# Rounding and spreading V on GpSimd, straight from fp32, in a softmax-times-V kernel

## Chip, cores, metric

One core of a Trainium2 chip. The metric is the device time of one execution in microseconds (us), lower is better. "Same" means less than 2% of difference.

## The reference

```python
batch, n_heads, seq, head_dim = 8, 12, 1024, 64      # scores 8x12x1024x1024 fp32, v 8x12x1024x64 fp32
attn = np.exp(scores - np.max(scores, axis=-1, keepdims=True))
attn = attn / (np.sum(attn, axis=-1, keepdims=True) + 1e-8)
return np.matmul(attn, v)
```

403 MB of scores, 25 MB of V and 25 MB of output have to cross between device memory and the core.

## The kernel before

The 96 heads run in 24 rounds of four. For each head, ScalarE takes the exponential of the scores (fp16 out; the maximum is not subtracted), TensorE transposes it into PSUM (the memory that its results go to), VectorE copies it back to SBUF (the main on-chip memory; `pt`), and TensorE multiplies with V. V carries a column of ones, so that the same product gives the row sums; VectorE divides by them. All transfers are issued by SyncE (SP in the profile), in program order, on one queue.

V is loaded for four heads at once, as fp32, each head on 32 partitions. GpSimd (POOL) rounds the whole tile to fp16, and VectorE (DVE) spreads each head with four copies onto all 128 partitions of that head's operand `vones`:

```python
v_sb = sb_pool.tile([P, C // L, S, L, D], FP32, name="v_sb")     # 128 x 2048
v_half = sb_pool.tile([P, C // L, S, L, D], FP16, name="v_half")
# vones_bufs: four tiles [P, C, D + 2] fp16, ones in the last columns

def cast_v():
    nc.gpsimd.tensor_copy(out=v_half[:], in_=v_sb[:])

def spread_v(k, s, behind=None):
    copy = nc.vector.tensor_copy(
        out=vones_bufs[k][s * Q : (s + 1) * Q, :, 0:D].rearrange("i (h l) d -> i h l d", l=L),
        in_=v_half[k * Q : (k + 1) * Q, :, s],
    )
    ...

def last(n0):                      # after the round's four heads
    with tc.If(n0 < BH - 2 * AHEAD) as cmp:
        load(AHEAD - 2, ...)       # third head of the next round; the first two were issued earlier
        load_v((n0 + 2 * AHEAD) % BH)
        load(AHEAD - 1, ...)       # fourth head
        store(n0, AHEAD - T)
    ...                            # the last two rounds load no V

def heads(n0):
    for k in range(AHEAD):
        if k == 0:
            for s in range(S):
                spread_v(k, s)
        for r in range(R):
            ...                    # exp, transposes, copy to pt
            if k < AHEAD - 1 and r % (R // S) == 0:
                spread_v(k + 1, r // (R // S), copy)
            ...                    # product of an earlier row group
    ...
    cast_v()
    last(n0)
```

## Time and profile before

| | before |
|---|---|
| time | 1065.75 us (1065.68 to 1065.76, three runs) |
| busy: TensorE, VectorE, ScalarE, GpSimd | 731, 787, 736, 48 us |
| DMA queue | 453 MB, 99.2% of the 16 engines' span |
| a steady round of four heads | 43.7 us, 18.87 MB, 432 GB/s |

In the page, a group's line gives line number, engine, operation, output and input, count, then busy time and mean ns of one, then the engine's idle time before it and what ended it. In a timeline, the first two numbers are start and length in us, and the bracket is the idle time before with what ended it. The lines themselves are in the prediction.

### The profile page before, as it was taken

What the parts mean: (1) busy time and instruction counts of PE and PEld (TensorE: products, weight loads), DVE (VectorE), ACT (ScalarE), POOL (GpSimd) and SP (SyncE); (2) the same over time, 40 slices, a digit from 0 to 9 for tenths busy, and PEclk for the clock granted to TensorE, in tenths of its full rate; (3) what the DMA queues carried; (4) which work ended last, traced back from release to release, by engine and by line L of the source; (5) the groups of instructions that cost most, each with busy time, mean ns of one, the idle gap of its engine ahead of it and who ended that gap; (6) DMA issues with size and microseconds to landing.
All of it is one profiled execution on the core that took longest, in us unless ns stands there. A gap on an engine that the chain in (4) does not pass through costs nothing.

```text
span 1064.0 us, 32161 instructions
## 1 busy us (share of the span) xinstructions
PE 731.4 (69%) x12288; PEld 678.4 (64%) x12288; DVE 786.6 (74%) x1589; ACT 735.6 (69%) x432; POOL 48.1 (5%) x31
## 2 busy tenths in 40 slices
PE   2766766767766677677686776867666777666676
PEld 2665756667666667666575665767565666666675
DVE  3776876868768777677786776868768687687777
ACT  3766776666767668586676866667766668676685
POOL 0000000000000000000000000000000000000000
PEclk9888888878889888888988888888889788898989
DMA  9999999999999999999999999999999999999995
GB/s 397 431 418 434 426 433 434 433 434 432 432 434 432 425 443 430 429 431 428 433 431 436 432 434 434 431 434 424 441 427 434 432 426 435 432 432 428 440 425 236
DMA packets 24772, 453.06 MB, mean 426 GB/s; under 512 B 2752, under 2 KB 2752, under 8 KB 9152
## 3 DMA queue, kind: packets, MB, share of 16 engines
q1 hardware_dynamic: 24768, 453.00, 99.2%
q8 instruction: 4, 0.07, 0.0%
HBM read 436.21 MB, written 25.17 MB: 434 GB/s over the span
## 4 chain that ended last, share of the span: by engine, by line
DMA 81%; ACT 12%; issue 3%; ACTq 1%; PE 1%; DVE 0%; SPq 0%; PEld 0%; DVEq 0%
DMA s_nat<-in_scores_dram 81%; ACT p_nat L255 12%; PE psT L267 1%; ACTq L255 1%; ACTq L226 0%; ACTq L292 0%; PE psO L145 0%; DVE pt L273 0%; PE psO_whole L145 0%; SPq L184 0%; PEld L267 0%; ACTq L320 0%; DVE out_sb L129 0%; SPq L196 0%; PEld L145 0%
## 5 line engine op out<-in xcount | busy, mean ns | idle before, releaser
L255 ACT ACTIVATE p_nat<-s_nat 128x2048 f16<-128x2048 f32 (+1 forms) x408 | 704.8, 1799 | 228.1 <-DMA s_nat<-in_scores_dram 202.2
L267 PE MATMUL psT<-order,p_nat 128*128 128x128 f16 x6144 | 574.9, 246 | 269.9 <-ACT p_nat L255 263.9
L273 DVE COPY pt<-psT 128x1024 f16<-128x1024 f16 x768 | 515.8, 687 | 200.6 <-PE L267 109.4
L267 PEld LDWEIGHTS <-p_nat 128*128 128x128 f16 x6144 | 446.5, 123 | 298.3 <-ACT p_nat L255 295.7
L145 PEld LDWEIGHTS <-pt 128*128 128x128 f16 x6144 | 302.9, 107 | 81.0 <-DVE pt L273 77.7
L145 PE MATMUL psO<-vones,pt 128*128 128x65 f16 x3072 | 177.4, 201 | 53.9 <-DVE pt L273 50.2
L145 PE MATMUL psO_whole<-vones,pt 128*128 128x65 f16 x3072 | 189.9, 211 | 2.7 <-DVE pt L273 2.4
L207 DVE COPY vones<-v_half 32x512 f16<-32x512 f16 x384 | 109.4, 285 | 22.8 <-POOL v_half L203 6.0
L255 ACT ACT_TABLE_LOAD x24 | 30.8, 1283 | 89.8 <-DMA s_nat<-in_scores_dram 81.7
L203 POOL CAST v_half<-v_sb 128x2048 f16<-128x2048 f32 x25 | 47.4, 1896 | 1002.3 <-DVE vones L207 957.1
L129 DVE TENSOR_TENSOR out_sb<-psO,recip 64x256 f32<-64x256 f32 x192 | 81.1, 423 | 6.1
L129 DVE TENSOR_TENSOR out_sb<-psO_whole,recip 64x512 f32<-64x512 f32 x96 | 66.1, 688 | 3.0
L124 DVE RECIPROCAL recip<-psO 128x4 f32<-128x4 f32 x96 | 17.1, 178 | 34.4 <-PE psO L145 17.6
L124 DVE RECIPROCAL recip<-psO_whole 128x8 f32<-128x8 f32 x48 | 9.7, 203 | 4.5 <-PE psT L267 3.9
L71 DVE MEMSET vones<- 128x16 f16 x4 | 0.2, 72 | 0.8 <-PEq L309 0.8
L62 DVE CAST order<-ident 128x128 f16<-128x128 f32 x1 | 0.2, 227 | 0.4 <-POOL ident masks.py:199 0.4
masks.py:199 POOL TENSOR_SCALAR_AFFINE_SELECT ident<-ident 128x128 f32<-128x128 f32 x1 | 0.3, 295 | 0.1
masks.py:197 POOL MEMSET ident<- 128x128 f32 x1 | 0.2, 205 | 0.3 <-POOLq L309 0.3
L309 POOL MEMSET const-float32-0.0<- 128x1 f32 x1 | 0.1, 100 | 0.2 <-issue 0.2
L309 POOL MEMSET const-bfloat16-1.0<- 128x1 bf16 x1 | 0.1, 103 | 0.0
L309 POOL MEMSET const-uint8-127<- 128x1 uint8 x1 | 0.1, 103 | 0.0
L309 POOL MEMSET const-float32-1.0<- 128x1 f32 x1 | 0.1, 100 | 0.0
## 6 DMA issues: line engine op xcount, KB each, us to landing
s_nat<-in_scores_dram SPq DMA_DIRECT2D x96, 4096.0 KB, 35.8
v_sb<-in_v_dram SPq DMA_DIRECT2D x24, 1024.0 KB, 33.1
out_dram<-out_sb SPq DMA_DIRECT2D x48, 512.0 KB, 26.9
s_nat<-in_scores_dram SPq DMA_DIRECT2D x3, 2048.0 KB, 32.4
s_nat<-in_scores_dram SPq DMA_DIRECT2D x1, 1024.0 KB, 25.4
s_nat<-in_scores_dram SPq DMA_DIRECT2D x2, 512.0 KB
```

The costliest lines, as they stand in the source:

```text
L62: nc.vector.tensor_copy(out=order16[:].rearrange("p (t j) -> p t j", t=T), in_=ident32[:].rearrange("p (j t) -> p t j", t=T),)
L71: nc.vector.memset(vo[:, :, D : D + 2], 1.0)
L124: nc.vector.reciprocal(out=recip, in_=psO[:, :, :, D : D + 1])
L129: nc.vector.tensor_tensor(out=rows.rearrange("j (b g) d -> j b g d", g=G), in0=psO[part, :, :, 0:D], in1=recip[part].to_broadcast([W, last ...
L145: nc.tensor.matmul(out=bank[:, g * M : (g + 1) * M], lhsT=pt[:, c * P : (c + 1) * P], rhs=st["vones"][:, c, 0:M], start=(c == 0), stop=(c ...
L203: nc.gpsimd.tensor_copy(out=v_half[:], in_=v_sb[:])
L207: copy = nc.vector.tensor_copy(out=vones_bufs[k][s * Q : (s + 1) * Q, :, 0:D].rearrange("i (h l) d -> i h l d", l=L), in_=v_half[k * Q : ( ...
L255: nc.scalar.activation(out=p_nat[:, g : g + rows, :].rearrange("p r (x v) -> p x r v", v=Q * L), in_=s_bufs[k][:, r + g : r + g + rows, :] ...
L267: nc.tensor.transpose(out=psT[:, c * P : (c + 1) * P], in_=p_row[:, c // L, c % L, :], identity=order16[:],)
L273: copy = nc.vector.tensor_copy(out=pt[:], in_=psT[:])
L309: nc = _bacc.Bacc("TRN2", target_bir_lowering=False, num_devices=1)
```

## The change

Its intent is to take V's handling off VectorE, the busiest engine, and to save the fp16 copy of the tile. GpSimd reads fp32 and writes fp16 into `vones`, four copies a head, after the head's last product.

```diff
-    v_half = sb_pool.tile([P, C // L, S, L, D], FP16, name="v_half")
...
-        if r == R - 1 and k == T - 1:
-            store(n0, 0)
+        if r == R - 1:
+            spread_v(k)
+            if k == T - 1:
+                store(n0, 0)
...
-    def cast_v():
-        nc.gpsimd.tensor_copy(out=v_half[:], in_=v_sb[:])
-    def spread_v(k, s, behind=None):
-        copy = nc.vector.tensor_copy(... in_=v_half[k * Q : (k + 1) * Q, :, s])
+    def spread_v(k):
+        for s in range(S):
+            nc.gpsimd.tensor_copy(... in_=v_sb[k * Q : (k + 1) * Q, :, s])
...
-            if k == 0:
-                for s in range(S):
-                    spread_v(k, s)
...
-                if k < AHEAD - 1 and r % (R // S) == 0:
-                    spread_v(k + 1, r // (R // S), copy)
...
-        cast_v()
         last(n0)
...
-    cast_v()
+    for k in range(AHEAD):
+        spread_v(k)
     load_v(AHEAD)
```

More of the change, by code (lines that the diff above doesn't have):

```diff
@@ L200, in load_v @@
         )
-    def cast_v():
-        nc.gpsimd.tensor_copy(out=v_half[:], in_=v_sb[:])
-    def spread_v(k, s, behind=None):
-        copy = nc.vector.tensor_copy(
-            out=vones_bufs[k][s * Q : (s + 1) * Q, :, 0:D].rearrange(
-                "i (h l) d -> i h l d", l=L
-            ),
-            in_=v_half[k * Q : (k + 1) * Q, :, s],
-        )
-        if behind is not None:
-            after(copy, behind)
+    def spread_v(k):
+        for s in range(S):
+            nc.gpsimd.tensor_copy(
+                out=vones_bufs[k][s * Q : (s + 1) * Q, :, 0:D].rearrange(
+                    "i (h l) d -> i h l d", l=L
+                ),
+                in_=v_sb[k * Q : (k + 1) * Q, :, s],
+            )
     def load_next(k, n0):
@@ L272, in heads @@
                 pt = take(pt_bufs)
-                copy = nc.vector.tensor_copy(out=pt[:], in_=psT[:])
-                if k < AHEAD - 1 and r % (R // S) == 0:
-                    spread_v(k + 1, r // (R // S), copy)
+                nc.vector.tensor_copy(out=pt[:], in_=psT[:])
                 if r == R - 1:
```

## The prediction

> **What bounds the kernel now.** I read the page from the top: busy times, slices, queues, the chain that ended last; then the traffic of one steady round of four heads; then the moments at which SyncE issues its transfers in that round.
>
> The page of the kernel before: busy times, the DMA row of the slices, the queue, the chain by engine, and the two groups that the change removes.
> ```profile
> PE 731.4 (69%) x12288; PEld 678.4 (64%) x12288; DVE 786.6 (74%) x1589; ACT 735.6 (69%) x432; POOL 48.1 (5%) x31
> ...
> DMA  9999999999999999999999999999999999999995
> ...
> q1 hardware_dynamic: 24768, 453.00, 99.2%
> ...
> DMA 81%; ACT 12%; issue 3%; ACTq 1%; PE 1%; DVE 0%; SPq 0%; PEld 0%; DVEq 0%
> ...
> L207 DVE COPY vones<-v_half 32x512 f16<-32x512 f16 x384 | 109.4, 285 | 22.8 <-POOL v_half L203 6.0 <-PE L267 3.2 <-DVE out_sb L129 2.1
> L203 POOL CAST v_half<-v_sb 128x2048 f16<-128x2048 f32 x25 | 47.4, 1896 | 1002.3 <-DVE vones L207 957.1 <-DMA v_sb<-in_v_dram 40.8 <-POOLq L292 4.3
> ```
> No compute engine is over 74% busy; the one queue is at 99.2% and full in every slice but the last. The chain gives DMA 81% and VectorE 0%.
>
> One round (two scores loads, a store, then a third scores load, V, the fourth scores load, a store), busy time by stretch; after the five engines come granted clock, DMA share and GB/s:
> ```profile
> 405.63:449.34 43.71, 30.59 (x504) 28.46 (x501) 32.48 (x67) 30.65 (x18) 1.90 (x1) 0.80 1.00 432
> 449.34:493.02 43.68, 31.55 (x510) 29.44 (x508) 32.73 (x67) 30.64 (x18) 1.90 (x1) 0.80 1.01 432
> ```
> A round moves 4 x 4.194 + 1.049 + 2 x 0.524 = 18.87 MB; over 43.68 us that is 432 GB/s. 24 rounds are 453 MB, 1048.6 us at that rate; the other 15 us or so are first transfer and tail.
>
> SyncE's timeline for the same round, then its longest waits (total, times, longest us):
> ```profile
> 437.92 0.34 SPq L184 DMA_DIRECT2D s_nat<-in_scores_dram  x1
> 442.85 0.33 SPq L196 DMA_DIRECT2D v_sb<-in_v_dram  x1
> 449.34 0.33 SPq L184 DMA_DIRECT2D s_nat<-in_scores_dram  x1
> 456.05 0.36 SPq L163 DMA_DIRECT2D out_dram<-out_sb  x1
> ```
> ```profile
> SPq L184 <- ACT p_nat L255: 273.4, 47, 13.1
> ...
> SPq L226 <- SPq L226: 129.6, 22, 9.1
> SPq L196 <- POOL v_half L203: 97.3, 23, 5.6
> ```
> The V load waits for the GpSimd cast, the fourth scores load for the last exp, the store for VectorE. SyncE works in order: what holds V holds the two behind it.
>
> **What the Trainium skill says.**
> - "DMA: Bandwidth & Descriptors", Specifications, gives an SBUF fabric ceiling of 435 GB/s for the 16 DMA engines. The 432 above agree: removing work from an engine cannot move these bytes faster.
> - "GPSIMD Engine Reference", 3.1 Elementwise, gives 1.03 cycles per element for short one-input bodies, and its Specifications 1.2 GHz. The old cast: 2048 x 1.03 / 1.2 = 1758 ns, traced 1896, so some 138 ns fixed. It agrees.
> - "VectorE: DVE Perf Modes", Why PSUM operands drop a tier: a PSUM operand rules out the modes that use both SBUF read ports. "SBUF — State Buffer", Who interferes with whom: only VectorE's two-port modes, or two SBUF inputs, block GpSimd, and DMA does not contend with compute engines. VectorE's remaining large work reads PSUM, so I expect no blocking of the new copies. The trace before has too little GpSimd work to show it.
>
> **The change, part by part.**
> 1. Removed from VectorE: 384 copies x 285 ns = 109.4 us. Busy time goes to about 677 us (64%). Off the path, as the chain says.
> 2. Removed from GpSimd: 25 casts, 47.4 us.
> 3. Added to GpSimd: 16 copies before the loop and 16 in each of 24 rounds, 400 in all. Each is 32 partitions x 512 elements, fp32 to fp16. Time per partition goes by elements: 512 x 1.03 / 1.2 + 138 = 577 ns (an estimate from the cast and the GPSIMD page). The build shows each copy also waiting for GpSimd's copy before it, so I allow 0.58 to 0.75 us. Per round 9 to 12 us of 43.7; in all 231 to 300 us, 22 to 28%.
> 4. Moved, and the point that matters: the fp32 V buffer is now free only after the last four copies of the round, which wait for the fourth head's last product to stop reading its V operand. Before, the cast ended at 442.71, in the middle of the fourth head. Now, from PE's timeline:
> ```profile
> 454.26 0.43 PE L145 MATMUL psO<-vones,pt 128*128 128x65 f16 x8 [1.20 <-DVE pt L273]
> ```
> The last product ends near 454.7; with 0.2 us for the semaphore and 4 x 0.58 to 0.75 us, V is free at 457.2 to 457.9. So V is issued near 457.6 instead of 442.85 (15 us later), the fourth scores load near 458.2 instead of 449.34 (9 us later), the store near 459 instead of 456.05.
>
> Does that drain the queue? Issue to landing for V here is 33.1 us, so V landed at 475.9; its own 1.049 MB take 2.4 us at 432 GB/s, so it started to move at about 473.5. The fourth load landed 36.0 us after its issue, at 485.4, which is 9.5 us after V: one 4.194 MB transfer at full rate, so they move one behind the other. Until 473.5 the queue has older transfers. Allow 1.4 us from issue to first byte: the last store, with nothing ahead, lands in 2.6 us, of which its 0.524 MB explain 1.2. Then V may be issued as late as 472.1 at no cost. **At 457.6 there are 14.5 us to spare.** The landing times stay; only the wait in the queue gets shorter: V from 33 to about 18 us, the fourth load from 36 to about 27.
>
> After the store, SyncE is held by its own wait at the end of the round's branch (the L226 line above), for earlier transfers to land; that ends near 462.3, when the second head's scores arrive and its exp starts. SyncE gets there by about 459.5 now, so the next round's first issue does not move. Loss per round: 0.
>
> 5. The new V (landed 475.9) is spread for heads 0 to 2 by about 486, and first used at 502 (458.56, the first product of a round, plus 43.7).
> 6. Start: V lands at about 5.7; 16 copies end at 15 to 17.7 instead of the cast's 7.6. The V load behind them delays SyncE's loop entry, which ScalarE waited for at 8.06. Its 1.28 us table load then ends at 16.5 to 19, against a first exp at 15.31: 1 to 4 us. Head 0's exp (7.3 us) ends by 26.5, head 1 by 34, and head 2's scores come at 36.1: caught up, while the queue holds loads until about 48.
> 7. End: the last two rounds load no V. GpSimd's last four copies end at about 1061, before the last store lands (1059.2 + 2.6 = 1061.8). The last head had no VectorE copies to lose. 0 to 0.5 us.
>
> Sum: -109.4 us and +184 to 253 us of busy work on two engines with room, 0 per round on the DMA queue, 0 to 0.5 us at the end: **1065.8 us**, the same.
>
> **Rivals.**
> - SyncE's order starves the DMA engines. For it: 9 us of delay in the fourth load, 22 rounds, would be 200 us if all were exposed. Against: the 14.5 us of spare time. It needs V later than 472.1, thus copies over (472.1 - 454.9) / 4 = 4.3 us each; at 5 us each, about 3 us a round, 1130 us.
> - GpSimd becomes the bound: 16 copies over 43.7 us need 2.7 us each, over four times my estimate. At 3 us, 48 us a round: about 1170 us. The move between partition groups (32k to 32s) is the one thing that the whole-tile cast did not show.
> - The freed VectorE time makes it faster. For it: VectorE was the busiest engine, at 74%. Against: 0% of the chain, and the DMA rate at its ceiling. At most about 1 us, near 1064.8.
>
> **Range and chances.** Runs before spread over 0.1 us; what can move are start and end, by one or two us: 1063.8 to 1068.5. For slower by over 2% a copy must be several times dearer than its element count says: 0.02. For faster by over 2%, 21 us would have to come out of a queue that is full for 1049 us: 0.01.
>
> **What would show it right or wrong.** Right: DMA share about 99%, 432 GB/s in a steady round, VectorE about 677 us, GpSimd 231 to 300 us with copies of 0.58 to 0.75 us, V's time to landing near 18 us, and SyncE waiting for GpSimd with no idle DMA behind it. Wrong: a copy over 2.7 us; V issued later than 17 us after the fourth head's last product; DMA share in a steady round under 0.97; or products waiting for GpSimd.

## The result

1065.00 us (1064.82 to 1065.37, four runs) against 1065.74 (1065.68 to 1065.76, four runs): ratio 0.9994, 95% interval 0.9976 to 1.0011, the same. A ratio is the mean time of one kernel's fast runs over that of the other's of the same rounds, so it is not quite the ratio of the medians quoted.

The page of the changed kernel: busy times, DMA row, queue, chain, and the new group on GpSimd.
```profile
PE 725.4 (68%) x12288; PEld 683.9 (64%) x12288; DVE 682.8 (64%) x1205; ACT 735.7 (69%) x432; POOL 244.5 (23%) x406
...
DMA  9999999999999999999999999999999999999995
...
q1 hardware_dynamic: 24768, 453.00, 99.3%
...
DMA 64%; PE 14%; ACT 5%; PEld 4%; DVE 4%; POOL 3%; issue 3%; SPq 1%; POOLq 1%; ACTq 0%
...
L206 POOL CAST vones<-v_sb 32x512 f16<-32x512 f32 x400 | 243.8, 610 | 815.1 <-PE psO L144 297.3 <-PE L261 242.5 <-PE psT L261 214.2
```
One round of it, from the fourth load's issue to the next; after the busy times of the five engines come granted clock, DMA share and GB/s:
```profile
457.65:501.33 43.68, 30.59 (x515) 28.97 (x512) 28.42 (x51) 30.66 (x20) 9.76 (x16) 0.81 1.01 432
```
VectorE lost 104 us and GpSimd gained 196; the queue is as full as before, at the same 432 GB/s. The chain looks quite different, although the time is not: DMA fell from 81% to 64%, and TensorE and GpSimd came in. The next two views tell why that is no new bound.

Part of one round in SyncE's timeline, then two of its waits (total, times, longest us):
```profile
456.95 0.33 SPq L197 DMA_DIRECT2D v_sb<-in_v_dram  x1
457.65 0.33 SPq L185 DMA_DIRECT2D s_nat<-in_scores_dram  x1
458.30 0.35 SPq L164 DMA_DIRECT2D out_dram<-out_sb  x1
463.80 6.45 SPq L185 DMA_DIRECT2D s_nat<-in_scores_dram  x2
```
```profile
SPq L197 <- POOL vones L206: 428.3, 23, 20.1
...
SPq L223 <- SPq L223: 71.7, 22, 6.6
```
V is issued at 456.95 instead of 442.85, the fourth load at 457.65 instead of 449.34, and SyncE's wait for GpSimd has grown from 97 to 428 us. Yet the next round's first load goes out at 463.80; before the change it was 463.76.

GpSimd's timeline in the same round:
```profile
454.18 2.63 POOL L206 CAST vones<-v_sb 32x512 f16<-32x512 f32 x4 [5.17 <-PE psO L144]
475.84 5.29 POOL L206 CAST vones<-v_sb 32x512 f16<-32x512 f32 x8 [19.03 <-PE L261]
```
The copies at 454.18 are the last head's and hold V back. Those at 475.84 start when the next V lands.

The chain of the changed kernel, in order of time, across that point:
```profile
453.40 0.64 PE psO L144 x8
...
456.20 0.62 POOL vones L206
456.95 0.33 SPq L197
...
457.65 27.77 DMA s_nat<-in_scores_dram
485.53 1.92 ACT p_nat L249
```
The chain follows releases: ScalarE was released by the load, the load could be issued once SyncE had issued V, V once GpSimd was done. It can't see that of the 27.8 us to landing 15 to 18 were spent waiting in the queue behind older transfers and V (one DMA engine had V whole at 472.94, the last at 475.69). The trace has the landings: V at 475.64 before and 475.69 now, the fourth load at 485.37 before and 485.43 now.

Last, the start of the fourth head's exp, from ScalarE's timelines of before and of the changed kernel, to the same effect:
```profile
441.79 7.41 ACT L255 ACTIVATE p_nat<-s_nat 128x2048 f16<-128x2048 f32 x5 [4.85 <-DMA s_nat<-in_scores_dram]
```
```profile
441.85 7.42 ACT L249 ACTIVATE p_nat<-s_nat 128x2048 f16<-128x2048 f32 x5 [4.84 <-DMA s_nat<-in_scores_dram]
```

### The profile page after: what moved, and what is told of

It reads as the page before. It is cut to its first block, busy times and chain, and to the rows that moved or that the text cites. A ratio compares the mean times of both kernels' runs of the same rounds, so it can differ in the third digit from the quotient of the medians.

```text
span 1063.0 us, 32824 instructions
## 1 busy us (share of the span) xinstructions
PE 725.4 (68%) x12288; PEld 683.9 (64%) x12288; DVE 682.8 (64%) x1205; ACT 735.7 (69%) x432; POOL 244.5 (23%) x406
## 4 chain that ended last, share of the span: by engine, by line
DMA 64%; PE 14%; ACT 5%; PEld 4%; DVE 4%; POOL 3%; issue 3%; SPq 1%; POOLq 1%; ACTq 0%
DMA s_nat<-in_scores_dram 64%; PE psT L261 7%; PE psO L144 5%; ACT p_nat L249 5%; DVE pt L267 4%; POOL vones L206 3%; PEld L261 2%; PEld L144 2%; PE psO_whole L144 1%; SPq L197 1%; SPq L185 0%; POOLq L206 0%; POOLq L223 0%; POOLq L284 0%; POOLq L312 0%
## 5 line engine op out<-in xcount | busy, mean ns | idle before, releaser
L261 PE MATMUL psT<-order,p_nat 128*128 128x128 f16 x6144 | 567.7, 248 | 261.7 <-ACT p_nat L249 258.5
L206 POOL CAST vones<-v_sb 32x512 f16<-32x512 f32 x400 | 243.8, 610 | 815.1 <-PE psO L144 297.3
L144 PEld LDWEIGHTS <-pt 128*128 128x128 f16 x6144 | 306.2, 107 | 89.8 <-DVE pt L267 86.9
L144 PE MATMUL psO<-vones,pt 128*128 128x65 f16 x3072 | 184.3, 203 | 58.5 <-DVE pt L267 58.2
## 6 DMA issues: line engine op xcount, KB each, us to landing
v_sb<-in_v_dram SPq DMA_DIRECT2D x24, 1024.0 KB, 18.3
s_nat<-in_scores_dram SPq DMA_DIRECT2D x3, 2048.0 KB, 32.4
```

What stands on the lines that cost most here:

```text
L144: nc.tensor.matmul(out=bank[:, g * M : (g + 1) * M], lhsT=pt[:, c * P : (c + 1) * P], rhs=st["vones"][:, c, 0:M], start=(c == 0), stop=(c ...
L206: nc.gpsimd.tensor_copy(out=vones_bufs[k][s * Q : (s + 1) * Q, :, 0:D].rearrange("i (h l) d -> i h l d", l=L), in_=v_sb[k * Q : (k + 1) * ...
L261: nc.tensor.transpose(out=psT[:, c * P : (c + 1) * P], in_=p_row[:, c // L, c % L, :], identity=order16[:],)
```

## The experiments

The theory: the full DMA queue bounds both kernels; V's later issue costs nothing because older transfers are still in the queue; VectorE's relief is real but hidden. The rivals: the later issue does cost time and VectorE's relief happens to pay it back; or the relief is worth nothing. And the prediction's 14.5 us to spare can be measured.

### How late may V be? late_small, late_large

The delay is GpSimd work that adds zero, so that results stay right: one call of `again` is four instructions.

```diff
         if r == R - 1:
             spread_v(k)
+            if k == AHEAD - 1:
+                for _ in range(2):         # late_large: 4
+                    again(k)               # vones[k] = v_sb + 0, four instructions
```

> The changed kernel, with eight more GpSimd instructions (add of zero, result unchanged) between the fourth head's four copies and the release of the fp32 V buffer. Estimate of one: the Trainium skill, GPSIMD Engine Reference, 3.1 Elementwise, has 4497 ns for 2048 two-input elements, so 1.1 to 1.3 us for 512; V is then issued some 9 to 11 us later than in the changed kernel (456.95 in its round), near 466 to 468. Theory (a full DMA queue hides the wait until V is issued later than about 471.5, 14.5 us of room): same time, 1065 us plus or minus 1, V's time to landing falls from 18 to 7 to 9 us. Rival (the delay costs time and is paid back by the VectorE relief): 10 us in 22 rounds, up to 220 us more, about 1285 us; at a tenth of that still 1087 us.

Measured: 1099.03 us (1094.30 to 1104.59), ratio 1.0326, slower. One added instruction took 1277 ns. The theory's "same time" **missed**. The rival's 1285 missed by far more, but its lower figure, 1087, came nearer than the theory. Part of it is in how the run was made: the last round too has the added work, and SyncE's last wait, for GpSimd, was 9.4 us. The rest is a real cost, about 1.1 us in each of 22 rounds, although V's time to landing, 7.4 us in the median, came as expected. The four runs fall in two groups, near 1094 and near 1104.

> As the run with eight, with sixteen of the added instructions: V issued 18 to 21 us later than in the changed kernel, past the room of 14.5 us. Theory: the round becomes the loop from V's issue over V and the fourth load landing, the fourth head's exp and products, and GpSimd's copies, back to V's issue: 29.1 us without a queue in the changed kernel's trace, plus 18 to 21, so 47 to 50 us against 43.7; 22 rounds, 75 to 140 us slower, 1140 to 1205 us, and idle DMA engines in front of V in each round (share 0.87 to 0.93). Rival (no such knee, GpSimd work is hidden whatever its place): 1065 us.

Measured: 1282.79 us (1281.19 to 1283.00), ratio 1.2028. The direction and the idle engines came as expected, the size did not, and the DMA share of 84.8% is under the expected 87 to 93%. The page of this run, the DMA row and the queue:
```profile
DMA  9989779798797887978979779797797977979790
...
q1 hardware_dynamic: 24768, 453.00, 84.8%
```
Some 20 us are the end again (SyncE waited 19.6 us there). A round, from one V issue to the next, took 53.2 us (503.89 to 557.10) where the sum had 50.6: V landed 4.8 us after its issue and the fourth load 10.8 us after V (9.7 at full rate), so the loop without any queue is near 31.6 us, not 29.1.

### late_5 and late_11: the same, without the end

The same instructions, now inside the branch that loads V, so that the last two rounds have none:

```diff
             load(AHEAD - 2, (n0 + (2 * AHEAD - 2)) % BH)
+            for _ in range(1):             # late_11: 2
+                again(AHEAD - 1)
             load_v((n0 + 2 * AHEAD) % BH)
```

> The changed kernel with four added GpSimd instructions (1.34 us apart in the first two late runs, so 5.4 us) before the release of V, but not in the last two rounds, which load no V, so that the kernel's end does not wait for them. The runs so far put the edge of the room below 10.8 us, against the 14.5 us of the prediction. Theory now (the room ends where the first DMA engine runs dry, 12 us after the changed kernel's V issue, less some 2 to 4 us in which a short queue already slows packets): 5.4 us are free, 1065 us plus or minus 1.5. Rival (every microsecond of delay costs a little, 0.08 us a round per us as in the run with eight): 0.4 us in 22 rounds, 9 us, 1074 us.

Measured: 1065.21 us (1064.97 to 1065.45), ratio 0.9994. V was issued at 462.13 in the round where the changed kernel has 456.95. So 5.2 us more are free.

> As the run with four, with eight (10.8 us), again not in the last two rounds. In the first run with eight, 1099 us, the trace shows the kernel's end waiting 9.4 us for GpSimd, and stretched DMA packets of some 18 us in all. Theory: without the end's wait 1083 to 1090 us, slower than before by 0.8 to 1.1 us a round, with no idle DMA engine but stretched packets. Rival (the 33 us were all in the end and in the last rounds): 1065 us.

Measured: 1080.19 us (1074.76 to 1084.47), ratio 1.0149: 15 us in 22 rounds, 0.7 us a round, a little under the range expected. The interval, 1.0109 to 1.0189, leaves no doubt of a loss. Again there are two groups, 1074.76 and 1076.13 against 1084.24 and 1084.47; the profile is of the first, so it shows the smaller loss. Why the groups differ, and why late_small lost more a round, is not settled. V's issue in two rounds of it, from SyncE's timeline, then the queue from the page:
```profile
520.71 0.33 SPq L199 DMA_DIRECT2D v_sb<-in_v_dram  x1
...
564.86 0.33 SPq L199 DMA_DIRECT2D v_sb<-in_v_dram  x1
```
```profile
q1 hardware_dynamic: 24768, 453.00, 99.3%
```
The two V issues are 44.15 us apart instead of 43.68, and yet the queue is as busy as in the changed kernel, with the same bytes.

Why does a delay of 10.8 us cost when 14.5 were thought to be free? The trace counts each transfer's landing in 16 steps, one per DMA engine. Taken from those counts, for the third scores load, which is the last transfer ahead of V:

```
                V issued   third load: first engine   last engine
before           442.85          470.49                  473.19
changed kernel   456.95          470.49                  473.25
late_5           462.13    (V's first 472.99, as before)
late_11          520.71          523.11                  525.98
```

The engines are not in step: the first is done 2.7 us before the last, and the prediction took the last. That leaves 12 us at most. The second part: in late_11 V came 2.4 us before the first engine was done, so hardly an engine ran dry, and still time was lost. The times that the packets of the queue took add up to 1065.0 us of all 16 engines, against 1055.7 in the changed kernel. That is 9.3 of the 9.7 us by which the profiled run is longer (1072.7 against 1063.0); only some 0.4 us are idle engines. Packets of 32 KB otherwise take 1.213 us; in late_11, 319 of 12032 took more than 1.3 us (26 in the changed kernel), half of these 1.58 us or more. They lie mostly 11 to 16 us after V's issue, and five of the rounds have about two thirds of the excess. So the loss in late_11 is stretched packets, not an empty queue. What stretches them is not settled. It is not GpSimd's added work: in late_11_v_last below, which has the same work, the packets add up to 1055.6 us. The runs show only that it happens when transfers are issued shortly before the engines need them.

### v_last, late_large_v_last, late_11_v_last: the order of issue

```diff
-            load_v((n0 + 2 * AHEAD) % BH)
             load(AHEAD - 1, (n0 + (2 * AHEAD - 1)) % BH)
+            load_v((n0 + 2 * AHEAD) % BH)
```

> The changed kernel, with the fourth scores load issued ahead of V. Theory: the fourth load goes back to its old issue moment, right after the last exp (about 449.3 in the round), and its time to landing back from 27.8 to about 34 us; V lands behind it, some 10 us later; total the same, 1065 us plus or minus 1. Rival (V's wait in front of the fourth load costs something): faster by more than 1 us.

Measured: 1065.03 us (1064.97 to 1065.22), ratio 0.9991. The fourth load now goes out at 450.47 and lands after 32.4 us. Seven microseconds earlier in the queue changed nothing, as expected.

> The sixteen added GpSimd instructions together with the fourth scores load ahead of V. Theory (it is SyncE's order of issue that carries the cost, not GpSimd's work): V is issued near 475 to 478, the next round's first load right after it, and the fourth load still moves until about 483, so the queue stays full or nearly so: 1065 to 1075 us, against 1140 to 1205 for the same GpSimd work with V in front. Rival (GpSimd's work or its SBUF traffic slows the kernel): as slow as the run with V in front.

Measured: 1134.15 us (1132.50 to 1136.93), ratio 1.0643: 149 us better than with V in front, but the expectation of at most 1075 **missed**. About 20 us are the end's wait as before (20.0 us here). The rest, some 49 us or 2.2 a round, fits the same limit at another place: in one round V was issued at 545.23, half a microsecond before the first DMA engine had done the fourth load (545.72), and the next round's first load at 547.90, when only the slowest engines (548.07) still had it. Here engines did run dry: the queue is busy for 96.0% of the span, and the end's wait is under 2% of it.

> The eight added GpSimd instructions of the run late_11, with the fourth scores load issued ahead of V. Theory: V is then issued near 469.3 in the round of the changed kernel (458.5 with no delay, plus 10.8) and the next round's first load near 471.5 to 472, while the fourth load, issued right after the last exp, keeps the engines at work until 482 to 485: 10 us of queue left at the tightest point, so no cost, 1065 us plus or minus 1.5, against 1080 with V in front. (With 21.5 us the same order left about 1 us of queue and cost some 2 us a round.) Rival (GpSimd's added work costs by itself): 1075 to 1085 us as in late_11.

Measured: 1065.04 us (1064.93 to 1065.17), ratio 0.9990, against 1080.19 for late_11, which has the same GpSimd work (on another chip, but the kernel before took 1065.94 and 1065.82 us beside the two). So that work costs nothing in itself. What costs is what SyncE may not issue while it waits for it.

### half_before, half_after: what the relief is worth

Inside the loop each scores load moves half of its rows (results wrong), in both kernels:

```diff
-            load(AHEAD - 2, (n0 + (2 * AHEAD - 2)) % BH)
+            load(AHEAD - 2, (n0 + (2 * AHEAD - 2)) % BH, (R // 2,))
...                                         # the other three loads alike
```

> The kernel before, with every scores load inside the loop cut to the first four of its eight row groups (the result is wrong on purpose; the other rows hold old scores). 10.5 MB a round are 24.3 us of DMA, so the queue is no longer the bound. Theory: VectorE (32.7 us busy a round, with some 2 us of gaps between instructions) becomes it: 34 to 37 us a round, 850 to 910 us. Rival (the time hangs on something other than DMA bytes): 1065 us.

> The changed kernel with the same cut of the scores loads. Theory (the relief of VectorE is real and only hidden by the DMA queue): VectorE has 28.3 us busy a round, ScalarE 30.7, so 31.5 to 34.5 us a round, 790 to 850 us, 4 to 10% faster than the kernel before with the same cut. Rival (GpSimd's new place in the chain costs as much as VectorE gains once the queue is short): the same as it or slower.

Measured: 859.31 us (859.10 to 860.06) and 822.34 us (821.95 to 824.77), in the same rounds: 37 us or 4.3% apart, both inside what was expected. The busy line and the queue of the two pages, before first:
```profile
PE 644.9 (75%) x12288; PEld 572.7 (67%) x12288; DVE 766.3 (89%) x1589; ACT 742.9 (87%) x432; POOL 48.1 (6%) x31
...
q1 hardware_dynamic: 24768, 264.25, 77.0%
```
```profile
PE 633.9 (77%) x12288; PEld 582.7 (71%) x12288; DVE 672.1 (82%) x1205; ACT 731.7 (89%) x432; POOL 243.6 (30%) x406
...
q1 hardware_dynamic: 24768, 264.25, 79.3%
```
With the queue at 77% VectorE is the busiest engine, and the change takes 94 us from it; ScalarE at 89% then stands in the way. So the gain exists, and the DMA queue hides it in the real kernel. The rival that a cost of V's later issue is paid back by it falls with v_last and late_5, where the fourth load goes out 7 us earlier, or V 5 us later, and the time stays, and with vector_back below, which has the later issue without the relief and takes 1.0 us more than the kernel before.

### vector_back, vector_less: the 0.7 us

vector_back is the changed kernel with VectorE's 16 copies a round back in their places, between tiles that nobody uses; vector_less is the kernel before without them (results wrong: all rounds use the first V).

```diff
+                if k < AHEAD - 1 and r % (R // S) == 0:
+                    dummy(k + 1, r // (R // S), copy)   # d_dst <- d_src, 32 x 512 fp16, VectorE
```

> The changed kernel with VectorE given back its 16 copies of 32 x 512 fp16 a round, in their old places, but from and to tiles that nobody else uses. Theory: the 0.7 us by which the changed kernel came out faster are the copies for the last heads, which pushed VectorE's work into the last head's tail; so 1065.7 us again, VectorE 790 us busy. If VectorE's SBUF copies and GpSimd's copies exclude each other (as the skill's SBUF page has it), those few that meet take up to 0.6 us longer, in an engine with room: no change in time. Rival (the 0.7 us are the start or the DMA rate): it stays at 1065.0.

> The kernel before without its 16 VectorE copies a round (they are done once ahead of the loop, so all rounds use the first four heads' V: wrong on purpose), GpSimd's whole-tile cast kept. Theory: VectorE's relief alone gives the 0.7 us: 1065.0 us. Rival (GpSimd's new place gives or takes something): 1065.7 us, the same as before.

Measured in the same rounds, before 1065.81 us: vector_less 1065.14 (1064.93 to 1065.78), vector_back 1066.78 (1066.46 to 1067.20). Both are "same", and both intervals of the ratio contain 1 (0.9981 to 1.0009 and 0.9995 to 1.0025), so what follows rests on medians and on the ends of the traces. Taking the copies away gives 0.7 us, with GpSimd's casts as they were (though they now start when V lands). Putting them back takes 1.8 more than the changed kernel (1065.00, from other rounds) and 1.1 more than expected; VectorE was busy for 811.5 us, not 790.

The end of the kernel before, from VectorE's timeline, and the last store from that of all engines:
```profile
1045.27 0.29 DVE L207 COPY vones<-v_half 32x512 f16<-32x512 f16 x1
...
1048.55 0.29 DVE L207 COPY vones<-v_half 32x512 f16<-32x512 f16 x1
...
1056.69 0.69 DVE L273 COPY pt<-psT 128x1024 f16<-128x1024 f16 x1
...
1059.22 0.36 SPq L163 DMA_DIRECT2D out_dram<-out_sb  x1
```
The same last copy and store in the changed kernel:
```profile
1056.05 0.69 DVE L267 COPY pt<-psT 128x1024 f16<-128x1024 f16 x1
...
1058.59 0.36 SPq L164 DMA_DIRECT2D out_dram<-out_sb  x1
```
In the last round the exps of the second and third heads run back to back (14.70 us from 1030.12), VectorE falls behind, and the copies for the next heads push its backlog into the last head. Without them the last `pt` copy and the last store come 0.6 us sooner.

In vector_back the copies meet GpSimd's. Its VectorE group, then the range of the group (min, median, max ns):
```profile
L219 DVE COPY d_dst<-d_src 32x512 f16<-32x512 f16 x384 | 133.8, 348 | 14.3 <-DVE out_sb L132 0.7
```
```profile
L219 DVE COPY d_dst<-d_src x384: 273/286/659, 3.9 to 1049.6; 32x512 f16<-32x512 f16 x192
```
The median is as before (285 ns in the kernel before), but single copies take up to 659 ns, mean 348. GpSimd's copies take 609 ns in the mean, with some up to 751 (616 at most in the changed kernel). The Trainium skill, "SBUF — State Buffer", Who interferes with whom, says that a VectorE instruction in one of its two-port modes and a GpSimd instruction exclude each other, the later one waiting for the whole instruction of the other. The trace does not name the mode, but it agrees: all 107 VectorE copies of more than 300 ns began while a GpSimd copy ran and ended 143 to 152 ns after it, and the seven GpSimd copies of more than 620 ns began while a VectorE copy ran. In the last round this delays VectorE further: its last `pt` copy there starts at 1057.56, 0.9 us after that of the kernel before. This is most of the extra 1.1 us. The change itself has no such meeting, because all of VectorE's SBUF-to-SBUF copies in the loop went.

### copy_forms: the price of one copy

21 GpSimd copies to unused tiles ahead of the first spread.

```diff
+    for _ in range(3):
+        nc.gpsimd.tensor_copy(out=f_dst[:, 0:1024], in_=f_src[:, 0:1024])
+        nc.gpsimd.tensor_copy(out=f_dst[:, 0:512], in_=f_src[:, 0:512])
+        nc.gpsimd.tensor_copy(out=f_dst[0:32, 0:512], in_=f_src[0:32, 0:512])
+        ...                            # 32 x 256; rows of 64 with a gap: in place, moved by 64 partitions, on 128
```

> The changed kernel with 21 GpSimd copies to unused tiles ahead of its loop, to time the copy by itself: 1024 and 512 elements on 128 partitions, 512 on 32, 256 on 32, and 512 elements written 64 at a time with a gap, in place, moved by 32 partitions, and on 128. The prediction had 577 ns for 32 x 512 (slope 0.858 ns an element, 138 ns fixed, from one size); measured 610. Theory: time goes by elements per partition, 512 cost the same on 32 and 128 partitions, and the rows of 64 with a gap and not the move of partitions add the 33 ns: about 577 for 512 flat, 610 for 512 in rows. Rival: moving partitions costs the 33 ns; or the fixed part is 170 ns whatever the form, then 512 flat costs 610 as well.

The copy that moves goes by 64 partitions (0 to 31 onto 64 to 95), not by 32 as this text has it.

The groups of GpSimd by form (L294 in place, L295 moved by 64 partitions, both in rows of 64 with a gap; L292 flat):
```profile
L290 POOL CAST f_dst<-f_src 128x1024 f16<-128x1024 f32 x3 | 3.1, 1036 | 0.0
L291 POOL CAST f_dst<-f_src 128x512 f16<-128x512 f32 x3 | 1.8, 613 | 0.2
...
L295 POOL CAST f_pad<-f_src 32x512 f16<-32x512 f32 x3 | 1.8, 607 | 0.2
L294 POOL CAST f_pad<-f_src 32x512 f16<-32x512 f32 x3 | 1.8, 605 | 0.2
L292 POOL CAST f_dst<-f_src 32x512 f16<-32x512 f32 x3 | 1.8, 603 | 0.1
...
L293 POOL CAST f_dst<-f_src 32x256 f16<-32x256 f32 x3 | 1.2, 393 | 0.1
```
Neither the rows nor the move nor the number of partitions makes more than about 10 ns of difference; the last rival holds. From 256 to 512 to 1024 elements the steps are 210 and 423 ns, 0.82 to 0.83 ns an element, and some 180 ns are fixed.

The run says one more thing. Its first exp started at 31.92 us instead of 18.05, because the loop's entry waited for these copies, and it took 1064.91 us all the same (one run). The start has nearly 14 us of room.

## Why the prediction was right, and where it was not

The time was right: 1065.8 predicted, 1065.0 measured, and for the reason given. Step by step:

1. VectorE 677 us predicted, 682.8 measured: the 109 us of copies went, and the `pt` copies, now less often back to back, took 690 ns instead of 687 (4 us in 768).
2. GpSimd 231 to 300 us, copies 0.58 to 0.75 us: 244.5 us in all, 0.61 us each, four in 2.62 us. The bare estimate of 577 ns took its fixed term, 138 ns, from one size and the page's slope; it measured some 180.
3. V's issue 457.6, fourth load 458.2, store 459: 456.95, 457.65 and 458.30. The last product began at 453.40 instead of 454.26, as VectorE was less behind.
4. Landings unmoved, V's time to landing about 18 us: 18.3. The fourth load's about 27: 27.8. The next round's first issue unmoved: 463.80. All as said.
5. **"At 457.6 there are 14.5 us to spare"** was wrong in size, and the rival that worked from it (copies of 4.3 us before it hurts) with it. Measured: 5.2 us more are free, 10.8 more cost 0.7 us a round. The failed terms are "until 473.5 the queue has older transfers", which is true only of the slowest engine (the first is free 2.7 us sooner), and the 1.4 us from issue to first byte, which does not cover the slower packets behind a late issue. A small misreading adds to it: this V took 32.8 us to land (475.64), 33.1 being the median of all, so that its own sum has 14.2 us.
6. The start: table load's end predicted at 16.5 to 19, first exp at 18.05, caught up by the third head. The copy_forms run shows more room than thought.
7. The end: "the last head had no VectorE copies to lose; 0 to 0.5 us" of loss was wrong in sign. The copies for earlier heads reached into the last head through VectorE's backlog; 0.6 to 0.7 us were gained, as in vector_less, within what the intervals there can tell. That is the rival "at most about 1 us, near 1064.8".
8. No blocking of GpSimd's copies: right, 601 to 616 ns. vector_back shows that there would have been some, had VectorE kept copies from SBUF.

## What to carry to other kernels

Work taken from the busiest engine was worth at most 0.7 of 1065 us here, where the DMA queue is full in every slice but the last; ask first which bytes could go. What mattered of this change was what it does to the moments of issue: find the transfer that waits for the moved work, and the ones behind it in the issuing engine's order, and put the one that may be late last. Count the room from the first DMA engine that runs out, not from the last landing, and leave several microseconds of it (here, of 12 us at most, 5.2 were free and 10.8 cost 0.7 us a round).

## What the Trainium skill lacked or had wrong

- "GPSIMD Engine Reference", 3.1 Elementwise: no fixed cost of a GpSimd copy is given. The runs show 393, 603, 1036 and 1896 ns for 256, 512, 1024 and 2048 elements a partition: about 0.83 ns an element (1.0 cycle at the page's 1.2 GHz, where it has 1.03) and 180 ns fixed; 32 or 128 partitions, and a move by 64 partitions, make about 10 ns of difference at most. A two-input add of 512 took 1277 ns.
- "DMA: Bandwidth & Descriptors", Queues, rings and completion order: the page tells that the engines of a transfer finish independently, but not by how much (here 2.7 us between the first and last engine of one load in the changed kernel). That packets take longer when the transfers were issued only shortly ahead is not told (late_11: 319 packets of 32 KB took over 1.3 us instead of 1.21, 9.3 us of all 16 engines with the smaller packets).
- The same page, Where 436 GB/s comes from, says that for transfers between HBM and SBUF the HBM side, about 358 GB/s, binds. Read alone, this is wrong for a kernel on one core: one core here moved 432 GB/s in a steady round. The same page's section Measured has the reason: its own higher figures are of a single core, and 358 is each core's part when two stream at once (no run here has two).
